# A second-product weight half in a weight room instead of a staging room, in a float32 four-layer trunk

## The chip, the core and the metric

The kernel runs on one core of one Trainium2 chip. The metric is the device time of one execution in microseconds (us). Engines are named as in the profile: PE is TensorE (PEld its weight loads), DVE is VectorE, ACT is ScalarE, POOL is GpSimd, SP is SyncE, which here only issues transfers. An engine works through its own instructions in the order in which they were recorded, and waits at an instruction until what it reads is there and the room it writes is free.

## The reference

A trunk of four layers over 512 tokens of width 1024: a mixer and a gated feed-forward in each, and a last norm.

```python
D_MODEL = 1024; SEQ = 512; DEPTH = 4
FFN_HIDDEN = -(-8 * D_MODEL // (3 * 256)) * 256          # 2816

def swiglu_ffn(h, w_gate_up, w_down):
    g, u = jnp.split(h @ w_gate_up, 2, axis=-1)
    return (jax.nn.silu(g) * u) @ w_down

def reference(x, ...):
    for layer in range(DEPTH):
        kind = layer % N_MIXERS          # 0: s5_mixer, 1: gla_mixer, 2: diff_attn_mixer
        h = rmsnorm(x, norm_mix[layer])
        ...
        x = x + mix.astype(x.dtype)
        h = rmsnorm(x, norm_ffn[layer])
        x = x + swiglu_ffn(h, ffn_w_gate_up[layer], ffn_w_down[layer]).astype(x.dtype)
    return rmsnorm(x, norm_final)
```

The change lies in `@ w_down` of the feed-forward of layers 2 and 3.

## The kernel before

**Precision.** Every float32 factor is split into a high part (a cast by ACT to the format that TensorE takes, line 420) and a low part (source minus high part, by DVE, line 428), and a product of two factors is three TensorE products: high by high, high by low, low by high. So each weight tile of 128 x 1024 that is loaded is cast once and subtracted once. The result lies in a "whl" room, of which there are five in rotation; a cast waits until TensorE has read what the room held before.

**The feed-forward.** `ffn` works through 11 blocks of 256 hidden columns. A block's gate and up halves are computed with seven products instead of eight (sums of weight quarters and of activations take the place of one). Its steps have names: one, five, six, two, seven, three, four for the products, gate2 for the scaling and silu of the second half (lines 786 and 789), times for the product of gate and up (line 748 in layer 2, 750 in layer 3) into a "raw" tile. In layer 2 the tokens stand in a turned order there, and a half of the raw tile needs both writes of times; in layer 3 the first token half is written early.

**The down groups.** In layers 2 and 3, which have no side work of earlier stages, blocks 0 to 3 and 4 to 7 are each followed by `seven_down`: their 1024 hidden columns times w_down, again by seven products (lines 1113 to 1210). The four quarters of the weights and their sums are named "11", "21", "1", "S", "3", "22"; each is two halves of 128 x 1024 (j = 0, 1). The operands from raw are named "11", "12", "2", "1", "3", "4", "22" (`parts`: a cast by ACT on line 1114, a subtraction by DVE on line 1116). The products come in this order, operand by weight, and the bank: 11 by 11 (a), 12 by 21 (d), 2 by S (a), 1 by 1 (c), 3 by 3 (a), 4 by 22 (c), 22 by S (a). A product is 24 matmuls of 128 x 512 on line 1125; its result is added to x on line 1134. So there are four groups in a run; the page and the rows call them by their times, about 1464, 1586, 1956 and 2076 us.

**Where loaded weights lie.** There are two kinds of rooms. Three *staging rooms* ("wst", line 409) serve, in rotation, whatever is split at once: a block's "11" and "3", and of a group "11", "21" and "22". A load into one waits until DVE has subtracted from what lay there three loads ago. Eight *weight rooms* hold what is kept or added to: they are a list, taken from the front by `slots.pop(0)` and given back at its end. In the trace they are called slot, halves (four rooms that held the sides) and gain. A block takes three (its "1", "22" and "21"), a group takes four at first ("1" and "S"), and two more for "3". Transfers into them are on lines 772 (blocks) and 1089 (groups); some are followed by an accumulating transfer of a second quarter on POOL's queue (lines 775 and 1098).

**The order.** Inside these layers the code is written in program order, and a scheduler places each engine's instructions by what they depend on and by that order; SP's loads can so stand far ahead of the code that asks for them, if their room is free. In `seven_down`, `weights` loads "1" and "S" while the group's last block is being computed, `sums` loads "11" and then "21" behind that block's last product, `before` splits both, and `products` does the rest: after the first product it loads "3".

Of the kernel before, what the change touches and what calls it, by code (L numbers as in the profile page):

```python
# [340 lines left out]
class Trunk:  # L341
# [730 lines left out]
    def seven_down(self, fp, slots, rooms, wd, b0, r, na, turn):  # L1072
# [4 lines left out]
        W, H, side = {}, {}, {}  # L1077
# [3 lines left out]
        def source(kh, nh):  # L1081
            return [self.wb_src(wd, at(kh, j), nh * 512) for j in range(2)]

        def load(name, kh, nh, plus=None, keep=False):
            W[name] = []
            for src in source(kh, nh):
                if keep:
                    w = slots.pop(0)[:].rearrange("p k n -> p (k n)").rearrange("p (k n) -> p k n", n=512)
                    nc.sync.dma_start(w, src)
                else:  # L1090
                    w = self.staged(src, 2, 512)[:]
                W[name].append(w)
            if plus:
                more(name, *plus)

        def more(name, kh, nh):
            for w, src in zip(W[name], source(kh, nh)):
                nc.gpsimd.dma_start(w, src, accum_op=ALU.add)

        def split(name):  # L1100
            H[name] = []
            for w in W[name]:
                hl = self.high(w, 2, 512)
                self.low(hl, w)
                H[name].append(hl)

        def freed(name):
            for w in W.pop(name):
                slots.append(w.rearrange("p k n -> p (k n)").rearrange("p (k n) -> p k n", n=256))

        def parts(name, pieces):
            side[name] = o = fp.tile([P, 2, 4, 256], F32R, tag="act", name="part", bufs=na)
            for ks, y in pieces:
                self.last["part high"] = nc.scalar.copy(o[:, 0, ks], y)
            for ks, y in pieces:
                self.last["part low"] = v.tensor_tensor(o[:, 1, ks], y, o[:, 0, ks].bitcast(F32), op=ALU.subtract)

        def product(name, w, banks, first):
            o, hls = side.pop(name), H.pop(w)
            for k in range(4):  # L1120
                hl = hls[k // 2]
                for t in range(2):
                    ts = slice(t * P, (t + 1) * P)
                    for n, (y, z) in enumerate(((0, 0), (0, 1), (1, 0))):
                        self.last["mm"] = nc.tensor.matmul(  # L1125
                            banks[t][:], o[:, y, k, ts], hl[:, z, k % 2],
                            start=first and not (k or n), stop=k == 3 and n == 2, skip_group_check=True,
                        )

        def add(m, d, banks, f):  # L1130
            for t in range(2):
                n = 2 * m + t
                xs = self.x[:, n, d * 512 : d * 512 + 512]
                v.scalar_tensor_tensor(xs, banks[t][:], f[:, n : n + 1], xs, op0=ALU.mult, op1=ALU.add)  # L1134
# [2 lines left out]
        us = []  # L1137

        def weights():
            load("1", 0, 1, (0, 0), True)  # L1140
            load("S", 1, 1, None, True)

        def early():
            parts("11", [(whole, part(0, 0))])
# [4 lines left out]

        def sums():  # L1150
            load("11", 0, 0)
            load("21", 1, 0)
            with self.tc.issue_after(self.last["low"].ins):
                for w, y in zip(W["1"], W["S"]):
                    v.tensor_tensor(y, w, y, op=ALU.add)
# [7 lines left out]
        def products():  # L1163
            self.flush()
            if turn:
                parts("12", [(whole, part(0, 1))])
                self.behind = {"silu": self.last["part high"], "scaled": self.last["part low"]}
            s1, s2, s4 = part(1, 0), part(0, 0), part(0, 1)
            for ks, y in us:
                v.scalar_tensor_tensor(s2[:, ks], y, -1.0, part(1, 1)[:, ks], op0=ALU.mult, op1=ALU.subtract)  # L1170
            self.behind = None
            a = [self.acc("a2") for _ in range(2)]
            product("11", "11", a, True)
            load("3", 0, 1, (1, 1), True)
            parts("2", [(whole, s2)])
            split("S")
            add(0, 0, a, r)
            nr = self.sp.tile([P, NT], F32, tag="ms4", name="nr", bufs=2)
            with self.tc.issue_after(self.last["part low"].ins):
                v.tensor_scalar_mul(nr[:], r[:], -1.0)  # L1180
            d = [self.sbank("d2") for _ in range(2)]
            product("12", "21", d, True)
            more("S", 1, 0)
            with self.tc.issue_after(self.last["part low"].ins):
                v.tensor_tensor(s4, s2, s4, op=ALU.add)
                v.tensor_tensor(s1, s1, part(1, 1), op=ALU.subtract)
            parts("1", [(whole, s1)])
            split("1")
            freed("1")
            load("22", 1, 1)  # L1190
            add(0, 0, d, r)
            product("2", "S", a, False)
            parts("3", us)
            split("3")
            freed("3")
            add(0, 1, a, nr)
            c = [self.acc("c2") for _ in range(2)]
            product("1", "1", c, True)
            parts("4", [(whole, s4)])
            split("22")  # L1200
            add(1, 1, c, r)
            product("3", "3", a, False)
            parts("22", [(whole, part(1, 1))])
            split("S")
            freed("S")
            add(1, 1, a, nr)
            product("4", "22", c, False)
            add(0, 1, c, r)
            product("22", "S", a, False)
            add(1, 0, a, r)  # L1210

        return {"early": early, "before": before, "sums": sums, "weights": weights, "products": products}

    def turn_x(self, r):
# [1922 lines left out]
```

## Time and profile before

| | |
|---|---|
| median of 3 runs | 2214.54 us (2212.77 to 2217.34) |
| profiled execution | 2214.04 us, its span 2212.3 us |
| busy in the span | PE 97%, PEld 88%, DVE 77%, ACT 53%, POOL 16% |
| granted TensorE clock, mean of the span | 0.996 |
| bytes moved, mean rate | 354.67 MB, 160 GB/s |
| line 1125, the groups' matmuls | 672 of the 15313 |

Rows of the time-ordered view give start and length in us, engine, line, operation, what is written from what, and in brackets the idle time of that engine ahead of it with what ended it. Rows of the chain of waits give start, length and what the chain passed through, DMA included, from a transfer's issue to its landing. Rows by stretch give for each engine the busy time and the count of instructions, then the clock that was granted to TensorE (1.00 is full speed), the share of the DMA engines' time and the rate. Matmuls overlap in their pipeline: 24 of them that are each shown as about 0.39 us follow one another every 0.23 us.

### The profile page before, as it was taken

Reading aid. Unit: us, or ns where it says so; the run is one execution under the profiler, and the core shown is the slowest. Engines: PE = TensorE matmul, PEld = TensorE weight load, DVE = VectorE, ACT = ScalarE, POOL = GpSimd, SP = SyncE. Lnnn points to the kernel's source line nnn. Section 1 sums busy time; section 2 is a strip of 40 time slices with the busy share of each in tenths; the row PEclk is TensorE's granted clock in tenths of the full one; section 3 lists DMA queues with packets and bytes.
Section 4 is the critical chain, followed back from the end, with each engine's and each line's share of the span. In section 5 each row is a group of like instructions: output and inputs, shape, how many; then the busy total and the mean of one; then the engine's idle time right before and its main releaser. Section 6 shows DMA issues by size and latency. Waiting matters only on the chain.

```text
span 2212.3 us, 38516 instructions
## 1 busy us (share of the span) xinstructions
PE 2150.6 (97%) x15313; PEld 1949.0 (88%) x15313; DVE 1702.6 (77%) x2580; ACT 1171.6 (53%) x1852; POOL 360.0 (16%) x467
## 2 busy tenths in 40 slices
PE   6999999999999999999999999999999999999998
PEld 5888989989988898999988888989899888979997
DVE  9965978777988597876745686988886975988885
ACT  8634645444665465564435786644554334655553
POOL 3401152340211010100002221211110000111100
PEclk9999999999999999999999999999999999999999
DMA  4356767665863676765337465988872555879762
GB/s 93 65 174 172 185 161 188 174 173 158 187 152 115 157 183 173 178 188 136 96 129 160 98 153 145 254 215 217 201 169 58 146 158 145 210 200 226 197 149 76
DMA packets 320101, 354.67 MB, mean 160 GB/s; under 512 B 71220, under 2 KB 253648, under 8 KB 319794
## 3 DMA queue, kind: packets, MB, share of 16 engines
q1 hardware_dynamic: 243362, 247.39, 36.6%
q0 software_dynamic: 76560, 104.82, 25.6%
q8 instruction: 121, 1.98, 0.4%
q14 instruction: 58, 0.48, 0.1%
HBM read 318.20 MB, written 18.75 MB: 152 GB/s over the span
## 4 chain that ended last, share of the span: by engine, by line
PE 77%; DVE 11%; ACT 4%; DMA 3%; issue 3%; POOL 1%; SPq 0%; DVEq 0%; POOLq 0%; ACTq 0%
PE a L594 19%; PE c L594 9%; PE acc L448 8%; PE acc L450 8%; PE acc L449 8%; PE d L594 5%; DVE whl L428 3%; PE a L1125 3%; PE y L1875 2%; PE acc L1911 2%; PE c L1125 2%; ACT whl L420 1%; PE s L2883 1%; DMA wst<-in_ffn_w_down_dram 1%; PE op L2916 1%
## 5 line engine op out<-in xcount | busy, mean ns | idle before, releaser
L428 DVE TENSOR_TENSOR whl<-wst,whl 128x1024 fp32r<-128x1024 f32 x252 | 306.5, 1222 | 196.8 <-ACT whl L420 195.4
L594 PE MATMUL a<-side,whl 128*128 128x256 f32 x3240 | 392.2, 277 | 5.1 <-DVE whl L428 3.3
L594 PEld LDWEIGHTS a<-side,whl 128*128 128x128 f32 x3240 | 378.7, 188 | 8.0 <-DVE whl L428 4.8
L420 ACT CAST whl<-wst 128x1024 fp32r<-128x1024 f32 x252 | 263.8, 1051 | 221.8 <-PE acc L450 117.0
L594 PE MATMUL c<-side,whl 128*128 128x256 f32 x2160 | 260.7, 277 | 2.0 <-DVE whl L428 1.6
L594 PEld LDWEIGHTS c<-side,whl 128*128 128x128 f32 x2160 | 252.5, 188 | 2.8 <-DVE whl L428 2.3
L428 DVE TENSOR_TENSOR whl<-slot,whl 128x1024 fp32r<-128x1024 f32 x121 | 147.2, 1221 | 45.7 <-ACT whl L420 45.6
L448 PE MATMUL acc<-whl,act 128*128 128x512 f32 x448 | 176.1, 394 | 0.5 <-ACT whl L420 0.5
L450 PE MATMUL acc<-whl,act 128*128 128x512 f32 x448 | 174.9, 390 | 0.0
L449 PE MATMUL acc<-whl,act 128*128 128x512 f32 x448 | 174.9, 390 | 0.0
L420 ACT CAST whl<-slot 128x1024 fp32r<-128x1024 f32 x121 | 126.7, 1052 | 86.7 <-DVE slot L850 29.7
L420 ACT CAST whl<-halves 128x1024 fp32r<-128x1024 f32 x103 | 107.9, 1051 | 85.9 <-DVE halves L850 43.1
L428 DVE TENSOR_TENSOR whl<-halves,whl 128x1024 fp32r<-128x1024 f32 x103 | 125.2, 1221 | 23.5 <-ACT whl L420 23.0
L594 PE MATMUL a<-sides,whl 128*128 128x256 f32 x1080 | 132.1, 278 | 1.6 <-DVE whl L428 1.0
L594 PE MATMUL d<-sides,whl 128*128 128x256 f32 x1080 | 131.7, 278 | 0.4 <-ACT whl L420 0.4
L594 PEld LDWEIGHTS a<-sides,whl 128*128 128x128 f32 x1080 | 127.8, 188 | 2.9 <-DVE whl L428 1.2
L594 PEld LDWEIGHTS d<-sides,whl 128*128 128x128 f32 x1080 | 127.7, 188 | 0.8 <-ACT whl L420 0.6
L775 POOL DMA_DIRECT2D wst<-in_ffn_w_gate_up_dram x44 | 56.9, 1294 | 295.6 <-DMA wst<-in_ffn_w_gate_up_dram 114.7
L448 PEld LDWEIGHTS acc<-whl,act 128*128 128x128 f32 x448 | 84.0, 188 | 18.7 <-ACT whl L420 0.7
L450 PEld LDWEIGHTS acc<-whl,act 128*128 128x128 f32 x448 | 84.1, 188 | 17.6
L449 PEld LDWEIGHTS acc<-whl,act 128*128 128x128 f32 x448 | 84.2, 188 | 16.6
L1125 PE MATMUL a<-whl,part 128*128 128x512 f32 x384 | 90.5, 390 | 2.2 <-DVE x L1134 1.8
(567 smaller groups left out, 4378.6 us busy)
## 6 DMA issues: line engine op xcount, KB each, us to landing
wst<-in_ffn_w_gate_up_dram SPq DMA_DIRECT2D x88, 512.0 KB, 5.3
wst<-in_ffn_w_down_dram SPq DMA_DIRECT2D x80, 512.0 KB, 4.7
slot<-in_ffn_w_gate_up_dram SPq DMA_DIRECT2D x67, 512.0 KB, 5.3
wst<-in_ffn_w_gate_up_dram POOLq DMA_DIRECT2D x44, 512.0 KB, 7.4
halves<-in_ffn_w_gate_up_dram SPq DMA_DIRECT2D x44, 512.0 KB, 5.6
wst<-in_s_w_glu_dram SPq DMA_DIRECT2D x32, 512.0 KB, 5.1
wst<-in_diff_w_qkv_dram SPq DMA_DIRECT2D x24, 512.0 KB, 3.9
slot<-in_ffn_w_gate_up_dram POOLq DMA_DIRECT2D x20, 512.0 KB, 9.3
```

What stands on the lines that cost most here:

```text
L420: self.last["high"] = self.nc.scalar.copy(hl[:, 0], w[:])
L428: self.last["low"] = self.nc.vector.tensor_tensor(hl[:, 1], w[:], hl[:, 0].bitcast(F32), op=ALU.subtract)
L448: mm(out, lh, rh, start=first, stop=False)
L449: mm(out, lh, rl, start=False, stop=False)
L450: self.last["mm"] = mm(out, ll, rh, start=False, stop=last)
L594: mm(o, *two, start=first and not (j or k or n), stop=k == 3 and n == 2, skip_group_check=True,)
L775: nc.gpsimd.dma_start(w[:], left.quarter(*plus, b), accum_op=ALU.add)
L1125: self.last["mm"] = nc.tensor.matmul(banks[t][:], o[:, y, k, ts], hl[:, z, k % 2], start=first and not (k or n), stop=k == 3 and n == 2, s ...
L1875: mm(yb[:, b], q[:, j, b], om[:, j // 2, bs(b)], start=False, stop=j == 3)
L1911: mm(accs[t][:], zT[:, m // 2, kk, t * P : (t + 1) * P], hl[:, m % 2, kk % 2], start=kk == 0 and m == 0, stop=kk == KT - 1 and m == 2,)
L2883: nc.tensor.matmul(ss[m][:], qs[:, m, ts], ks[:, m, z], start=z == 0, stop=z == 1)
L2916: nc.tensor.matmul(op[:, 0], aT[:, kt], vall[0][:, kt, j * P : (j + 1) * P], start=kt == 0, stop=kt == 3)
```

## The change

Of the weights "21" of a down group, the second half (j = 1) is loaded into a weight room, taken from the front of the list. The first half stays in a staging room. `keep`, until now yes or no for both halves, becomes the set of halves that get a weight room. The room is given back behind the group's first product in program order, before "3" takes its two. All else is the same; `freed` gets a second argument, from which half on it gives back.

```diff
-        def load(name, kh, nh, plus=None, keep=False):
+        def load(name, kh, nh, plus=None, keep=()):
             W[name] = []
-            for src in source(kh, nh):
-                if keep:
+            for j, src in enumerate(source(kh, nh)):
+                if j in keep:
                     w = slots.pop(0)[:].rearrange("p k n -> p (k n)").rearrange("p (k n) -> p k n", n=512)
                     nc.sync.dma_start(w, src)
                 else:
...
-        def freed(name):
-            for w in W.pop(name):
+        def freed(name, n=0):
+            for w in W.pop(name)[n:]:
                 slots.append(w.rearrange("p k n -> p (k n)").rearrange("p (k n) -> p k n", n=256))
...
         def weights():
-            load("1", 0, 1, (0, 0), True)
-            load("S", 1, 1, None, True)
+            load("1", 0, 1, (0, 0), (0, 1))
+            load("S", 1, 1, None, (0, 1))
...
             load("11", 0, 0)
-            load("21", 1, 0)
+            load("21", 1, 0, None, (1,))
...
             product("11", "11", a, True)
-            load("3", 0, 1, (1, 1), True)
+            freed("21", 1)
+            load("3", 0, 1, (1, 1), (0, 1))
             parts("2", [(whole, s2)])
```

Since a line is added, lines from 1174 on have a number higher by one in the kernel of the change.

SP's loads around the first group, before. wst_15272 and wst_15274 are the halves of "11", wst_15276 and wst_15278 those of "21", wst_15386 and wst_15388 those of "22"; the second of the two loads in the second row and the one into gain are "3"; lines 772 and wst_15553 belong to the next block.

```order
L409 DMA wst_15272<-in_ffn_w_down_dram 128x2x512
L1089 DMA halves_14151<-in_ffn_w_down_dram 128x2x512 x2
L409 DMA wst_15274<-in_ffn_w_down_dram 128x2x512
L772 DMA halves_14151<-in_ffn_w_gate_up_dram 128x4x256
L409 DMA wst_15276<-in_ffn_w_down_dram 128x2x512
L1089 DMA gain_13567<-in_ffn_w_down_dram 128x2x512
L772 DMA halves_14151<-in_ffn_w_gate_up_dram 128x4x256
L409 DMA wst_15278<-in_ffn_w_down_dram 128x2x512
L409 DMA wst_15386<-in_ffn_w_down_dram 128x2x512
L409 DMA wst_15388<-in_ffn_w_down_dram 128x2x512
L409 DMA wst_15553<-in_ffn_w_gate_up_dram 128x4x256
```

And in the change:

```order
L409 DMA wst_15272<-in_ffn_w_down_dram 128x2x512
L1089 DMA halves_14151<-in_ffn_w_down_dram 128x2x512 x2
L409 DMA wst_15274<-in_ffn_w_down_dram 128x2x512
L1089 DMA halves_14151<-in_ffn_w_down_dram 128x2x512
L409 DMA wst_15276<-in_ffn_w_down_dram 128x2x512
L1089 DMA gain_13567<-in_ffn_w_down_dram 128x2x512
L772 DMA halves_14151<-in_ffn_w_gate_up_dram 128x4x256
L409 DMA wst_15385<-in_ffn_w_down_dram 128x2x512
L409 DMA wst_15387<-in_ffn_w_down_dram 128x2x512
L409 DMA wst_15552<-in_ffn_w_gate_up_dram 128x4x256
L772 DMA halves_14151<-in_ffn_w_gate_up_dram 128x4x256
```

The second load of the second row is now the second half of "21". The halves of "3" are the two single loads on line 1089: the one into gain as before, the other in the room and place that the next block's "1" had. The next block's "1" has the place of its "22", and its "22" comes behind the staged loads, into the room that "21" gives up.

DVE at the same place, before. whl_15282 and whl_15285 are the low parts of "11", whl_15288 and whl_15291 those of "21", whl_15337 and whl_15340 those of "S"; part_15299 is operand "12".

```order
L428 TENSOR_TENSOR whl_15285<-wst_15274,whl_15285 128x1024
L428 TENSOR_TENSOR whl_15288<-wst_15276,whl_15288 128x1024
L878 TENSOR_TENSOR r2_15153<-c_15095,r2_15153 128x512
L748 TENSOR_TENSOR raw_15014<-r2_15153,r1_15093 128x64x4 x2
L428 TENSOR_TENSOR whl_15291<-wst_15278,whl_15291 128x1024
L786 TENSOR_TENSOR g2_15294<-a_15065,R_14598 128x512
L428 TENSOR_TENSOR whl_15337<-halves_14151,whl_15337 128x1024
L748 TENSOR_TENSOR raw_15014<-g2_15294,r5_15123 128x64x4 x2
L1170 SCALAR_TENSOR_TENSOR raw_14801<-s3_14899,raw_15014 128x2x256
L428 TENSOR_TENSOR whl_15340<-slot2_14331,whl_15340 128x1024
L1116 TENSOR_TENSOR part_15299<-raw_15014,part_15299 128x1024
```

And in the change:

```order
L428 TENSOR_TENSOR whl_15284<-wst_15274,whl_15284 128x1024
L428 TENSOR_TENSOR whl_15287<-wst_15276,whl_15287 128x1024
L878 TENSOR_TENSOR r2_15153<-c_15095,r2_15153 128x512
L428 TENSOR_TENSOR whl_15290<-halves_14151,whl_15290 128x1024
L748 TENSOR_TENSOR raw_15014<-r2_15153,r1_15093 128x64x4 x2
L786 TENSOR_TENSOR g2_15293<-a_15065,R_14598 128x512
L428 TENSOR_TENSOR whl_15336<-halves_14151,whl_15336 128x1024
L748 TENSOR_TENSOR raw_15014<-g2_15293,r5_15123 128x64x4 x2
L1170 SCALAR_TENSOR_TENSOR raw_14801<-s3_14899,raw_15014 128x2x256
L428 TENSOR_TENSOR whl_15339<-slot2_14331,whl_15339 128x1024
L1116 TENSOR_TENSOR part_15298<-raw_15014,part_15298 128x1024
```

The low part of the second half of "21" reads a weight room (halves) and stands ahead of the first pair of raw products instead of behind it; the rest keeps its order.

## The prediction

> **What bounds the kernel now.** I read the page first, then the stretches of the four seven-product down groups, then TensorE's own order of time in them, and last the chain of waits.
>
> ```profile
> span 2212.3 us, 38516 instructions
> PE 77%; DVE 11%; ACT 4%; DMA 3%; issue 3%; POOL 1%; SPq 0%; DVEq 0%; POOLq 0%; ACTq 0%
> ```
>
> TensorE carries 77% of the chain that ended last, so a change helps where TensorE stands idle or runs slowly, and nowhere else. The change touches the four groups alone. Busy times by stretch, one row for each group (us; PE, weight load, DVE, ACT, POOL busy, granted clock, DMA share, GB/s):
>
> ```profile
> 1463.60:1508.40 44.80, 40.85 (x171) 32.98 (x170) 38.37 (x44) 21.91 (x23) 6.27 (x5) 0.92 0.86 213
> 1585.70:1627.70 42.00, 40.20 (x170) 32.49 (x169) 37.50 (x43) 21.90 (x23) 6.24 (x5) 0.96 0.89 214
> 1955.90:1999.60 43.70, 40.05 (x170) 31.16 (x169) 38.20 (x43) 20.44 (x22) 6.22 (x5) 1.00 0.89 216
> 2076.30:2114.40 38.10, 38.10 (x171) 31.55 (x170) 36.87 (x41) 20.55 (x22) 6.27 (x5) 1.00 0.87 213
> ```
>
> The fourth group has no gap: seven products in 38.10 us, 5.44 us each, 0.227 us for each of 24 matmuls. Against it the first loses 6.7 us, the second 3.9, the third 5.6, together 16.2 us. That is the ceiling of any change to these waits. TensorE's rows show where it is lost (start, length, what, idle before it and what ended that):
>
> ```profile
> 1457.26 2.88 PE L594 MATMUL c<-side,whl 128*128 128x256 f32 x24
> ...
> 1463.61 5.62 PE L1125 MATMUL a<-whl,part 128*128 128x512 f32 x24
> 1473.18 8.15 PE L1125 MATMUL d<-whl,part 128*128 128x512 f32 x24 [3.95 <-ACT part L1114]
> 1481.16 5.60 PE L1125 MATMUL a<-whl,part 128*128 128x512 f32 x24
> ...
> 1592.36 1.20 PE L1125 MATMUL d<-whl,part 128*128 128x512 f32 x4 [1.07 <-ACT part L1114]
> 1594.28 6.38 PE L1125 MATMUL d<-whl,part 128*128 128x512 f32 x20 [0.73 <-DVE part L1116]
> 1600.50 5.60 PE L1125 MATMUL a<-whl,part 128*128 128x512 f32 x24
> ...
> 1965.95 2.76 PE L1125 MATMUL d<-whl,part 128*128 128x512 f32 x11 [0.76 <-DVE whl L428]
> 1970.17 0.70 PE L1125 MATMUL a<-whl,part 128*128 128x512 f32 x2 [1.47 <-DVE x L1134]
> ```
>
> All of it lies at the second product (bank d) and, in the third group, in the products behind it. The releasers named are ACT and DVE. The chain of waits says what held those:
>
> ```profile
> 1460.14 6.80 DMA wst<-in_ffn_w_down_dram
> 1467.04 1.06 ACT whl L420
> ...
> 1472.08 1.05 ACT part L1114
> ...
> 1581.33 4.74 DMA wst<-in_ffn_w_down_dram
> 1586.17 1.06 ACT whl L420
> ...
> 1955.08 8.41 DMA wst<-in_ffn_w_down_dram
> 1963.59 1.05 ACT whl L420
> ```
>
> In three groups of four the root is one transfer: the second half of weights "21". Its staging room comes free only when the first half of "11" has been split, so it starts at 1460.14 and ACT's cast of it stands until 1467.04. On ACT and DVE everything behind that cast is late with it: the last block's gate (L786), its product into raw (L748), and from that the operand "12" of the second product (L1114 and L1116).
>
> **The change part by part.** (1) *The half moves to a weight room.* SyncE's rows in the first group:
>
> ```profile
> 1435.00 3.83 SPq L1089 DMA_DIRECT2D halves<-in_ffn_w_down_dram  x2
> 1450.22 0.37 SPq L772 DMA_DIRECT2D halves<-in_ffn_w_gate_up_dram  x1
> 1454.40 0.37 SPq L1089 DMA_DIRECT2D gain<-in_ffn_w_down_dram  x1
> 1455.54 0.37 SPq L772 DMA_DIRECT2D halves<-in_ffn_w_gate_up_dram  x1
> 1460.14 3.23 SPq L409 DMA_DIRECT2D wst<-in_ffn_w_down_dram  x3
> ```
>
> The second of the two issues of the first row (1435.00 + 3.83 - 0.37 = 1438.46) was the first half of "3". In the order of the change "21"'s second half has that place and that room. It goes out 21.7 us before 1460.14; with the 6.80 us of its landing it is there by 1445.3, before any cast of it can run: the cast writes a split room that the last block's product "three" reads until 1457.26 + 2.88 = 1460.1. The transfer leaves the path entirely.
>
> (2) *What is then next on the path, first group.* DVE's rows:
>
> ```profile
> 1462.90 0.68 DVE L878 TENSOR_TENSOR r<-c,r 128x512 f32<-128x512 f32 x1
> 1463.62 1.08 DVE L748 TENSOR_TENSOR raw<-r,r 128x256 f32<-128x256 f32 x2
> 1468.12 1.23 DVE L428 TENSOR_TENSOR whl<-wst,whl 128x1024 fp32r<-128x1024 f32 x1 [3.42 <-ACT whl L420]
> 1469.27 0.68 DVE L786 TENSOR_TENSOR g<-a,R 128x512 f32<-128x512 f32 x1
> 1473.82 1.22 DVE L1116 TENSOR_TENSOR part<-raw,part 128x1024 fp32r<-128x1024 f32 x1
> ```
>
> In the new order the low half of "21" (1.15 us from start to start) stands ahead of the raw pair, right behind L878. So L786 starts at 1463.5 + 1.15 + 1.05 = 1465.7 in place of 1469.27: 3.6 us earlier. It needs the last block's product, which ends as the group begins, at 1463.6, so nothing else holds it. What follows L786 has the same order on DVE and moves with it: ACT's part "12" to 1468.5, the first matmul of d to 1469.6, the end of L1116 (1473.82 + 1.22 = 1475.04) to 1471.4. TensorE is done with the first product at 1463.61 + 5.44 = 1469.05. Of 3.95 us of idle time 0.5 stays, four matmuls run, a wait of about 1.0 for L1116 stays, and the other 20 take 20 x 0.227 = 4.5: the third product starts at 1476.0 instead of 1481.16. Gain 5.1 us.
>
> Part of that is clock. While d ran, TensorE was granted half its speed:
>
> ```profile
> 1477.00:1478.00 1.00, 1.00 (x4) 0.81 (x3) 1.00 (x3) 0.00 (x0) 0.00 (x0) 0.50 0.99 180
> ```
>
> Group averages of 0.92 and 0.96 (rows above) say that the first lost 44.8 x 0.08 = 3.6 us of clock (idle time among them) and the second 42.0 x 0.04 = 1.7; the second fell after gaps of only 1.07 + 0.73 us, the third, at 1.00, did not in spite of similar ones. I take it that the remaining 0.5 + 1.0 us does not set it off; what it costs otherwise is a rival below. The Trainium skill (TensorE: Matmul & The Clock Gate, Part 1) says that the clock falls after an idle window of about 3.4 us. The second group's rows differ from that: 1.8 us of idle time in two pieces was enough. By the page the sum is the one below, by that row up to 3.4 us less.
>
> (3) *Second group.*
>
> ```profile
> 1584.09 0.68 DVE L878 TENSOR_TENSOR r<-c,r 128x512 f32<-128x512 f32 x1
> 1588.40 0.68 DVE L786 TENSOR_TENSOR g<-a,R 128x512 f32<-128x512 f32 x1
> ```
>
> By the same step L786 starts at 1584.7 + 1.15 + 1.05 = 1586.9, 1.5 us earlier. The first matmul of d moves from 1592.36 to 1590.9, which is before TensorE is ready (1585.7 + 5.44 = 1591.1), so that gap closes; the wait for L1116 ends at 1592.8 in place of 1594.28, and 20 matmuls at full clock end at 1597.4 instead of 1600.50. Gain 3.1 us.
>
> (4) *Third group.* Its operand "12" doesn't hang on the last gate, so d starts on time; the late half stops it in its middle and puts DVE behind.
>
> ```profile
> 1957.31 1.22 DVE L428 TENSOR_TENSOR whl<-wst,whl 128x1024 fp32r<-128x1024 f32 x1
> 1964.67 1.23 DVE L428 TENSOR_TENSOR whl<-wst,whl 128x1024 fp32r<-128x1024 f32 x1 [4.41 <-ACT whl L420]
> 1969.95 1.21 DVE L1116 TENSOR_TENSOR part<-raw,part 128x1024 fp32r<-128x1024 f32 x1
> ```
>
> DVE stands 4.41 us, and from 1964.67 it sets TensorE's pace. With the half there, DVE runs through from 1957.31 and all behind is 4.4 to 4.5 us earlier: L1116 would end at about 1967.3 (one add of 0.7 us now stands ahead of it), where TensorE wants the third product at 1955.9 + 10.9 = 1966.8. The next two products keep small waits, since DVE still sets them. Gain 4.5 of the 5.6 lost.
>
> (5) *Fourth group:* nothing to gain. *Free by cover:* the half of "3" that gives up its place now starts with the room that comes free at 1450.22; the next block's first sum (that row before) takes the place of the 1455.54 row, and that one, the next block's "22", goes out after the low half of "21", about 1465. These two are used only for the next block, which TensorE begins where the group ends, at 1508.40, and "3" for the fifth product; so 6 us of transfer and, for the two sums, 6 more of accumulation lie beside TensorE's products. If that cover were gone, it is the last rival. Splits, adds and matmuls are the same in number; one staging room fewer is used in a group, so the next staged loads start no later.
>
> Sum: 5.1 + 3.1 + 4.5 + 0 = 12.7 us. Both bounds: nothing below 0 gain by this step alone, at most 16.2. Against the profiled execution's own 2214.04 us (span 2212.3) it gives 2201.3; the median of the runs lies 0.5 higher, and I round to **2202**.
>
> **The rivals.** *The clock still falls* in the first and second group: the second group's 1.7 us in each, 2202 + 3.4 = 2205. For it speaks the second group now, against it the third.
>
> *Another transfer takes its place:* the first half of "21" still goes through a staging room, and starts after the last block's "3" is split. If the traffic that is now earlier made it land 3 us later, its cast would hold the same queue; three groups would give back up to 9 us: 2211. Against: as many bytes move as before, and 21.7 us of lead is far more than was missing.
>
> *Nothing happens:* if the room were not free at 1438, or the late operand hung on the last block's gate alone, the time stays at 2214. Against: the room took a load at that moment already, and DVE's 3.42 us ended with the cast.
>
> *Slower: "3" comes late.*
>
> ```profile
> 1481.41 1.05 ACT L420 CAST whl<-halves 128x1024 fp32r<-128x1024 f32 x1 [1.69 <-PE d L1125]
> ...
> DMA to landing us min/median/max: 3.4/5.7/14.8
> ```
>
> ACT's casts of "3" come from this row's place on, which would now be 1476.3, with the operand of the product in bank c behind them on ACT. The half needs two transfers, the load from 1450.2 and the accumulation on POOL's queue behind it (1.2 us of issue). At median landings it is there at 1462.8, 13.5 us early. It decides only when the two landings pass 25 us together; with the longest, 14.8 twice, it is there at 1481.0, 4.7 us late, in all four groups 18.8: 2221.
>
> **How the numbers follow.** Forecast 0.72, clock 0.11, another transfer 0.07, nothing 0.05, slower 0.05. The likeliest gives 2202; its own range is 2198.3 (all 16.2 us) to 2205. To hold eight of ten I leave out the top of the "another transfer" case, the unchanged and the slower one: 2198 to 2210. Differences under 0.2% (4.4 us) can't be told from none here. Faster by more than that means under 2210.1: the first two cases and some of the third, 0.87. Same: 0.08. Slower: 0.05.
>
> **What would show it.** After the change the chain of waits should have no staging transfer of w_down at 1460, 1581 and 1955; ACT's cast of "21"'s second half should read from a weight room with no wait for DMA; idle time before d should be under 1 us in the first group and none in the second; the clock should read 1.00 over all four groups, and these should last about 39.7, 38.9, 39.2 and 38.1 us. Wrong it is if d's idle time stays with another releaser, if the clock falls again, or if ACT waits for the rooms of "3" at 1476.

## The result, and the profile after

The changed kernel takes 2202.94 us (median of 4 runs, 2199.88 to 2204.37), beside 2214.26 (2212.77 to 2217.34) for the kernel before: a ratio of 0.9945, 95% interval 0.9928 to 0.9962. It is faster by 8 to 16 us; 2202 was predicted. Timed twice more beside experiments it took 2202.92 (ratio 0.9944, 0.9931 to 0.9956) and 2204.16 (0.9948, 0.9936 to 0.9961). Four executions of the experiments, with a mean clock of only 0.56 to 0.77, are left out of all medians and ratios here.

The head of the page and the chain of waits by engine, of the changed kernel:

```profile
span 2198.2 us, 38512 instructions
PE 79%; DVE 12%; ACT 4%; issue 2%; DMA 2%; POOL 0%; SPq 0%; DVEq 0%; POOLq 0%; ACTq 0%
```

The span is 14.1 us shorter, with the same number of matmuls (15313). The four groups by stretch (columns as in the prediction):

```profile
1463.10:1502.70 39.60, 38.70 (x171) 31.37 (x170) 37.93 (x44) 20.95 (x22) 7.54 (x6) 1.00 1.03 255
1580.00:1618.90 38.90, 38.44 (x171) 31.51 (x170) 37.24 (x44) 21.10 (x22) 6.54 (x6) 1.00 1.02 244
1946.30:1985.50 39.20, 38.93 (x171) 31.30 (x170) 38.12 (x43) 19.84 (x21) 6.71 (x6) 1.00 1.05 252
2062.10:2100.20 38.10, 38.10 (x170) 31.56 (x169) 36.06 (x41) 20.17 (x22) 6.26 (x5) 1.00 1.00 238
```

From the first matmul of a group to the first behind it, the groups went from 44.75, 42.03, 43.70 and 38.10 us to 39.60, 38.85, 39.21 and 38.09. That is 12.8 us; the clock, 0.92 and 0.96 in the first two, is 1.00 in all. Of the other 1.3 us of the span, 0.55 lies ahead of the first group (it starts at 1463.06 in place of 1463.61) and 0.8 between the second and third, where the change has nothing; further profiled executions of the same kernel had spans of 2201.2 and 2199.9, so this is what one execution differs from the next. In the three groups the chain of waits holds no transfer of w_down any more, where the prediction had found one in each (1460, 1581 and 1955 us).

TensorE in order of time, first group, then second, then third:

```profile
1463.06 5.65 PE L1125 MATMUL a<-whl,part 128*128 128x512 f32 x24
1468.89 1.19 PE L1125 MATMUL d<-whl,part 128*128 128x512 f32 x4 [0.18 <-ACT part L1114]
1470.80 4.83 PE L1125 MATMUL d<-whl,part 128*128 128x512 f32 x20 [0.72 <-DVE part L1116]
1475.46 5.60 PE L1125 MATMUL a<-whl,part 128*128 128x512 f32 x24
...
1585.46 1.07 PE L1125 MATMUL d<-whl,part 128*128 128x512 f32 x4
1586.99 4.83 PE L1125 MATMUL d<-whl,part 128*128 128x512 f32 x20 [0.46 <-DVE part L1116]
1591.65 5.60 PE L1125 MATMUL a<-whl,part 128*128 128x512 f32 x24
...
1957.17 5.86 PE L1125 MATMUL a<-whl,part 128*128 128x512 f32 x24
1962.87 5.90 PE L1125 MATMUL c<-whl,part 128*128 128x512 f32 x24
1969.04 5.72 PE L1125 MATMUL a<-whl,part 128*128 128x512 f32 x24 [0.27 <-DVE x L1134]
```

The wait of 3.95 us ahead of bank d is 0.18, that of 1.07 is gone, and from the first matmul of d to the next product it is 6.57 us (1468.89 to 1475.46, 0.72 of them idle) instead of 7.98 (1473.18 to 1481.16). SyncE, ACT and DVE of the first group show why:

```profile
1434.83 3.83 SPq L1089 DMA_DIRECT2D halves<-in_ffn_w_down_dram  x2
...
1458.90 1.04 ACT L420 CAST whl<-wst 128x1024 fp32r<-128x1024 f32 x1
1459.84 1.05 ACT L420 CAST whl<-halves 128x1024 fp32r<-128x1024 f32 x1
...
1475.71 1.05 ACT L420 CAST whl<-gain 128x1024 fp32r<-128x1024 f32 x1 [1.66 <-PE d L1125]
1478.38 1.06 ACT L420 CAST whl<-halves 128x1024 fp32r<-128x1024 f32 x1 [0.68 <-PE a L1125]
...
1462.26 0.68 DVE L878 TENSOR_TENSOR r<-c,r 128x512 f32<-128x512 f32 x1
1462.86 1.21 DVE L428 TENSOR_TENSOR whl<-halves,whl 128x1024 fp32r<-128x1024 f32 x1
1463.99 1.09 DVE L748 TENSOR_TENSOR raw<-r,r 128x256 f32<-128x256 f32 x2
1464.91 0.68 DVE L786 TENSOR_TENSOR g<-a,R 128x512 f32<-128x512 f32 x1
...
1469.53 1.22 DVE L1116 TENSOR_TENSOR part<-raw,part 128x1024 fp32r<-128x1024 f32 x1
```

The second issue of the first row, at 1434.83 + 3.83 - 0.37 = 1438.29, is now the second half of "21". ACT casts it at 1459.84 right behind the first half, with no wait in brackets. DVE's 3.42 us in front of its low part are gone, and L786 runs 3.8 us sooner measured from the group's start (1464.91 - 1463.06 = 1.85 in place of 5.66). The two casts of "3" (gain and halves, the third and fourth ACT rows) waited for TensorE, not for a transfer.

### The profile page after: what moved, and what is told of

It is laid out like the page before. It is cut to its first block, busy times and chain, and to the rows that moved or that the text cites. A ratio compares the mean times of both kernels' runs of the same rounds, so it can differ in the third digit from the quotient of the medians.

```text
span 2198.2 us, 38512 instructions
## 1 busy us (share of the span) xinstructions
PE 2145.4 (98%) x15313; PEld 1946.0 (89%) x15313; DVE 1702.5 (77%) x2580; ACT 1173.0 (53%) x1852; POOL 360.9 (16%) x467
## 4 chain that ended last, share of the span: by engine, by line
PE 79%; DVE 12%; ACT 4%; issue 2%; DMA 2%; POOL 0%; SPq 0%; DVEq 0%; POOLq 0%; ACTq 0%
PE a L594 20%; PE c L594 9%; PE acc L448 9%; PE acc L450 9%; PE acc L449 9%; PE d L594 5%; DVE whl L428 4%; PE a L1125 3%; PE y L1876 2%; PE c L1125 2%; PE acc L1912 2%; PE s L2884 1%; ACT whl L420 1%; PE op L2917 1%; PE tp L117 1%
## 5 line engine op out<-in xcount | busy, mean ns | idle before, releaser
L428 DVE TENSOR_TENSOR whl<-wst,whl 128x1024 fp32r<-128x1024 f32 x248 | 301.6, 1221 | 184.4 <-ACT whl L420 181.4
```

The source lines that it names most:

```text
L428: self.last["low"] = self.nc.vector.tensor_tensor(hl[:, 1], w[:], hl[:, 0].bitcast(F32), op=ALU.subtract)
```

## The experiments

The theory: the one transfer came late because its staging room came free late; what counts is when it lands. The rivals put to the test: that the weight room or the lighter rotation of the staging rooms does it whenever the transfer goes out; that either half would do, or both would do more; that the clock is the larger part; that only one layer gains. Each kernel was timed beside the kernel before on the same chip.

**The transfer held back to its old moment.** The room is the change's, but one element of it is written behind the first low part of "11", and the load is asked for behind that write (it overwrites the element):

```diff
@@ split, after the change
+                if name == "11" and j == 0:
+                    with self.tc.issue_after(self.last["low"].ins):
+                        v.memset(W["21"][1][:, 0, 0:1], 0.0)
+                    nc.sync.dma_start(W["21"][1], source(1, 0)[1])
@@ sums, after the change
-            load("21", 1, 0, None, (1,))
+            a, b = source(1, 0)
+            w = slots.pop(0)[:].rearrange("p k n -> p (k n)").rearrange("p (k n) -> p k n", n=512)
+            W["21"] = [self.staged(a, 2, 512)[:], w]
```

> The half keeps its weight room, as in the change, but its transfer is made to wait for the split of the first half of "11", as it did in the staging room: one element of the room is set on VectorE behind that split, and the load goes out behind it. Theory (only the moment of the transfer counts): the four groups last again about 44, 41.5, 43.5 and 38.1 us and the time is that of before to within 3 us, 2211 to 2215; the chain of waits runs again through that load. Rival (one load fewer in the staging rotation, or the other rooms of the later loads, give the gain): the groups stay at 39.6, 38.9 and 39.2 and the time at 2203.

Measured: 2221.62 us, ratio 1.0024 (1.0013 to 1.0035), with groups of 45.79, 46.48, 46.59 and 38.36 us. The whole gain is gone, and more. SyncE, the chain of waits and TensorE of this kernel, first group:

```profile
1459.78 0.37 SPq L409 DMA_DIRECT2D wst<-in_ffn_w_down_dram  x1
1460.40 0.37 SPq L1109 DMA_DIRECT2D halves<-in_ffn_w_down_dram  x1
...
1460.40 9.79 DMA halves<-in_ffn_w_down_dram
...
1474.74 7.25 PE L1129 MATMUL d<-whl,part 128*128 128x512 f32 x24 [5.88 <-ACT part L1118]
```

The transfer went out at the old moment (1460.40, against 1460.14), but 0.62 us behind a staged load of "22" that had not stood ahead of it before, and took 9.79 us in place of 6.80. So it landed 1470.19 - 1463.24 = 6.95 us after the group's start, where it had been 1466.94 - 1463.61 = 3.33, and the wait ahead of d grew to 5.88. In the second and third group, too, it went out 0.62 us behind a staged load and took about 3 us more (7.99 in place of 4.74, 11.12 in place of 8.41). The direction is the theory's, but the time lies outside the 2211 to 2215 that it gave: the experiment held only the issue fixed, and not the landing. Nor did it hold DVE's order: L786 stands ahead of the late low part here (1464.19 and 1471.36), which is why d is 1.9 us later than before and not 3.6.

**Held back, but sooner.** The same, with the write one split earlier, ahead of the first cast of "11", so that the load goes out ahead of "22".

```diff
@@ split, against the kernel above
             for j, w in enumerate(W[name]):
+                if name == "11" and j == 0:
+                    with self.tc.issue_after(self.last["low"].ins):
+                        v.memset(W["21"][1][:, 0, 0:1], 0.0)
+                    nc.sync.dma_start(W["21"][1], source(1, 0)[1])
                 hl = self.high(w, 2, 512)
                 self.low(hl, w)
                 H[name].append(hl)
-                if name == "11" and j == 0:
-                    with self.tc.issue_after(self.last["low"].ins):
-                        v.memset(W["21"][1][:, 0, 0:1], 0.0)
-                    nc.sync.dma_start(W["21"][1], source(1, 0)[1])
```

> As in late, the second half of "21" lies in a weight room and its transfer is held back, but the write that holds it stands one split earlier on VectorE (ahead of the low part of the first half of "11", not behind it), so that the transfer goes out about 1.2 us sooner and, on SyncE, ahead of the first staged load of "22" and not behind it. If the moment of the landing sets the time: issued near 1458.8, landed after 4.7 to 6.8 us at 1463.5 to 1465.6, 1.4 to 3.5 us sooner than in the kernel before; the first group 40.5 to 43.3, the second 39 to 40.7, the third 39.5 to 42.3 us, the median 2204 to 2211. If the kind of room matters: as the change, 39.6, 38.9 and 39.2, about 2203. If whatever goes out at that moment lands as late as in late (9.8 us, not for the load ahead of it): 1468.6, groups near 46, 44 and 45, about 2218.

Measured: 2215.01 us (2212.53 to 2220.38), ratio 0.9997 (0.9988 to 1.0006): no change, where the theory had 2204 to 2211 and the shortest of 11 runs is above that. The profiled execution is the longest of them, 5.4 us above their median, with groups of 45.09, 44.58 and 45.22, so in the others they may well be shorter. Its chain and DVE in the first group, then ACT and TensorE in the third:

```profile
1461.47 6.84 DMA halves<-in_ffn_w_down_dram
...
1469.49 1.23 DVE L428 TENSOR_TENSOR whl<-halves,whl 128x1024 fp32r<-128x1024 f32 x1 [3.46 <-ACT whl L420]
1470.63 1.07 DVE L748 TENSOR_TENSOR raw<-r,r 128x256 f32<-128x256 f32 x2
1471.55 0.67 DVE L786 TENSOR_TENSOR g<-a,R 128x512 f32<-128x512 f32 x1
...
1967.69 1.04 ACT L420 CAST whl<-halves 128x1024 fp32r<-128x1024 f32 x1 [10.09 <-DMA halves<-in_ffn_w_down_dram]
1968.64 1.04 ACT L1118 CAST part<-raw 128x1024 fp32r<-128x1024 f32 x1
...
1969.74 1.22 PE L1129 MATMUL d<-whl,part 128*128 128x512 f32 x2 [3.37 <-ACT part L1118]
```

In the first group the half did land sooner: 1461.47 + 6.84 - 1466.05 = 2.26 us after the group's start, 1.07 before its old place. But L786 stands at 5.50 from the start, against 5.66: the raw pair (L748), which ran ahead of the waiting low part in the kernel before, now stands behind it and takes 0.9 of that back. In the second group the half landed 0.95 us after the start, where it had been 0.40, and the same order makes d late by 2.47 us where it was 1.07. In the third group it landed 0.74 us sooner, but operand "12" (L1118 here) is behind ACT's wait of 10.09 us, and d starts 3.37 us late where it had been on time. In the kernel before that operand was cast and subtracted ahead of the late half, as its ACT and DVE show (the half's own cast and low part stand at 1963.59 and 1964.67):

```profile
1957.43 1.06 ACT L1114 CAST part<-raw 128x1024 fp32r<-128x1024 f32 x1 [4.57 <-DVE raw L750]
...
1959.04 1.22 DVE L1116 TENSOR_TENSOR part<-raw,part 128x1024 fp32r<-128x1024 f32 x1
```

So the moment of the landing is not all: the change also alters what is queued behind the half. Its order is the better one only if the half is there.

**The other half, and both.** The first half of "21" in the weight room and the second staged; then both halves in weight rooms, so that nothing of "21" is staged.

```diff
-            load("21", 1, 0, None, (1,))
+            load("21", 1, 0, None, (0,))
...
-            freed("21", 1)
+            slots.append(W.pop("21")[0].rearrange("p k n -> p (k n)").rearrange("p (k n) -> p k n", n=256))
```

> The first half of "21" goes to the weight room and the second stays in staging. Then the staged half takes the room of the last block's "3", which comes free some 7 us before that of "11", and should land before its cast is due. Theory: as the change, 2201 to 2205, groups 39.6, 38.9, 39.2 and 38.1. Rival (the next late transfer takes the place: the load that starts when the block's "3" is split is late by a little too, and now the half that the product needs last is not the early one): one or more groups longer by over 0.5 us, ACT waiting for DMA at the second cast of "21".

```diff
-            load("21", 1, 0, None, (1,))
+            load("21", 1, 0, None, (0, 1))
...
-            freed("21", 1)
+            freed("21")
```

> Both halves of "21" in weight rooms, none in staging. Theory: the first half was in time in the change already, so nothing is gained: 2201 to 2205, and the groups within 0.3 us of 39.6, 38.9, 39.2, 38.1. Rival (the first half's staged load is the next bound, as in the second group before, where ACT waited 1.15 us for it): the second and third group are shorter by 0.5 us or more each. Other rival (eight rooms are too few for six halves and the block's three, so "3" and the next block's sums come late): longer, with ACT or DVE waiting for a DMA into a weight room.

Measured: 2202.86 us, ratio 0.9936 (0.9924 to 0.9948), groups 39.61, 38.84, 38.91 for the other half; 2203.49 us, ratio 0.9940 (0.9928 to 0.9951), groups 40.97, 38.86, 39.08 for both. It doesn't matter which half moves: the one that stays in staging then has a staging room early enough. Moving both brings nothing more; the second and third group stayed within the 0.3 us expected, the first did not. SyncE, ACT and TensorE of the kernel with both, first group:

```profile
1457.69 0.37 SPq L1089 DMA_DIRECT2D gain<-in_ffn_w_down_dram  x1
...
1467.02 1.05 ACT L420 CAST whl<-gain 128x1024 fp32r<-128x1024 f32 x1 [3.15 <-DMA gain<-in_ffn_w_down_dram]
...
1474.09 1.20 PE L1125 MATMUL d<-whl,part 128*128 128x512 f32 x4 [1.57 <-ACT part L1114]
```

The second half got the room "gain", which comes free late (its load went out at 1457.69, where the change's went out at 1438.29), and ACT waits for it as it had for the staging room: a shortage of one kind of room had begun to turn into one of the other. It cost 1.4 us, in one group. This is the rival of too few rooms, in a small size, and it shows that a weight room that comes free late costs what a staging room does.

**The clock alone.** The kernel before, with 24 matmuls of 128 x 128 that nobody reads, into a spare bank, in the gap ahead of d in the first group and 6 in the second. They keep TensorE busy and shorten no wait.

```diff
@@ products, the kernel before
             d = [self.sbank("d2") for _ in range(2)]
+            if turn:
+                with self.tc.issue_after(self.last["mm"].ins):
+                    self.warmed(6 if b0 else 24, self.tp("warm")[:].rearrange("p a b -> p (a b)"))
             product("12", "21", d, True)
```

> The kernel before, with matmuls of no use in the gap ahead of the second product in layer 2: 24 of 128x128 in the first group (about 0.11 us each, 2.7 us of a gap of 3.95) and 6 in the second (0.7 of 1.07), to keep the clock up. If the falling clock is its own part of the loss: the clock reads 1.00 in both groups, the second product runs its last 20 matmuls in 4.5 to 4.8 us, and the groups last 43.2 instead of 44.8 and 40.3 instead of 42.0, 2211 in all. If the clock has no part: 44.8 and 42.0 or longer.

Measured: 2215.06 us, ratio 0.9992 (0.9983 to 1.0001), the first groups 44.31 and 41.14 us. The kernel before by stretch, in its two slow pieces; then this kernel in the same places, and TensorE's rows of the first:

```profile
1471.00:1478.00 7.00, 4.82 (x11) 3.50 (x12) 6.97 (x11) 3.49 (x4) 2.39 (x2) 0.52 0.90 188
1594.00:1597.40 3.40, 3.12 (x7) 2.48 (x8) 3.40 (x6) 0.20 (x1) 0.68 (x1) 0.52 1.10 190
```

```profile
1472.00:1478.00 6.00, 6.00 (x53) 5.86 (x51) 5.72 (x8) 4.51 (x6) 1.20 (x1) 1.00 0.89 234
1478.00:1484.40 6.40, 5.85 (x28) 4.53 (x27) 6.40 (x9) 2.23 (x3) 1.20 (x1) 1.00 0.92 160
...
1472.71 5.52 PE L1580 MATMUL warm<-ident 128*128 128x128 f32 x48
1477.98 0.71 PE L1125 MATMUL d<-whl,part 128*128 128x512 f32 x2
1479.24 5.28 PE L1125 MATMUL d<-whl,part 128*128 128x512 f32 x22 [0.55 <-DVE part L1116]
1484.36 1.98 PE L1125 MATMUL a<-whl,part 128*128 128x512 f32 x8
```

The clock stays at 1.00, and from the first matmul of d to the next product it is 6.38 us (1477.98 to 1484.36) where it was 7.98 (1473.18 to 1481.16); in the second group 7.05 where it was 8.14. So at full clock d takes 1.6 and 1.1 us less, although it waits for L1116 there (0.55 us, and 1.19 in the second group, where the kernel before had no wait and 0.73): a slow d had hidden part of that wait. The dummy work overran the gap (24 of them are 48 records and 5.27 us, twice what was reckoned; the gap is 3.95), so the group as a whole shows little of it, and the groups expected, 43.2 and 40.3, were missed: this sizes the clock's share, and is no way to get it.

**One layer at a time.** The change in layer 2 alone (the first two groups), then in layer 3 alone.

```diff
-            load("21", 1, 0, None, (1,))
+            load("21", 1, 0, None, (1,) if turn else ())
...
-            freed("21", 1)
+            freed("21", 1 if turn else 2)
```

`turn` is set in layer 2; for layer 3 alone both lines have `not turn`.

> The change in the two groups of layer 2 alone. Theory, by the terms of the sum: 5.1 + 3.1 = 8.2 us faster than before, and the third group at 43.7 again. Rival (the gain is one of the whole rotation of rooms and not of each group): the third group is shorter too, or the first two longer than 40.

> The change in the two groups of layer 3 alone. Theory: 4.5 us faster than before, the first two groups at 44.8 and 42.0 and the third at 39.2. Rival as for layer 2; and if the fourth group has anything to give, over 4.5 us.

Measured: 2206.27 us, ratio 0.9955 (0.9943 to 0.9968), for layer 2; 2209.88 us, ratio 0.9977 (0.9968 to 0.9986), for layer 3. By stretch, layer 2 alone and then layer 3 alone, first to third group:

```profile
1463.30:1503.00 39.70, 38.71 (x170) 31.45 (x170) 38.04 (x45) 20.95 (x22) 7.54 (x6) 1.00 1.02 251
1580.30:1619.20 38.90, 38.44 (x170) 31.51 (x170) 37.24 (x44) 21.12 (x22) 6.70 (x6) 1.00 0.99 238
1946.70:1989.10 42.40, 39.80 (x171) 31.18 (x169) 38.12 (x43) 20.44 (x22) 6.22 (x5) 1.00 0.89 218
```

```profile
1464.40:1510.60 46.20, 41.23 (x170) 33.23 (x169) 38.22 (x44) 21.89 (x23) 6.75 (x6) 0.93 0.86 213
1588.00:1629.90 41.90, 40.24 (x170) 32.49 (x169) 37.47 (x43) 21.91 (x23) 6.24 (x5) 0.96 0.89 213
1958.50:1997.70 39.20, 38.97 (x171) 31.29 (x170) 38.11 (x43) 19.84 (x21) 6.43 (x6) 1.00 1.07 250
```

Each group has the change's time where the change is, and none of it where it is not. The unchanged groups differ from one execution to the next with the landing of the half: the first is 46.20 us here (landing 7.94 us) and 44.75 in the profile before (6.80), the third 42.4 (7.22) and 43.70 (8.41). In the kernel with the dummy matmuls, where layer 3 is as before, the third is 41.84 (6.87), so a third group shorter than 43.7 is no effect of the change in layer 2. Against 2216.01 us of the kernel before, the intervals are 7.1 to 12.6 us and 3.1 to 7.1; the prediction's terms for them, 5.1 + 3.1 = 8.2 and 4.5, lie inside. No group's gain needs the change in the other layer, as a sum of terms requires.

**The wait that is left.** The change, with the splits of "S" placed behind those of operand "12" in layer 2, so that DVE reaches L1116 two low parts (2.3 us) sooner.

```diff
@@ products, the change
                 self.behind = {"silu": self.last["part high"], "scaled": self.last["part low"]}
+                twelve = self.behind
...
             parts("2", [(whole, s2)])
+            self.behind = twelve if turn else None
             split("S")
+            self.behind = None
```

> The change, and in layer 2 the splits of "S" stand behind the low part of operand "12" on VectorE and behind its high part on ScalarE. This is the wait that is now last ahead of the second product (0.72 and 0.46 us in the first two groups). Theory (VectorE's order sets what is left): that wait closes, the first group lasts 38.3 to 38.9 and the second 38.1 to 38.5, about 1.3 us in all, too little for the times to tell. Rival (the splits of "S" are then late for the third product): the wait moves to the product behind, and the groups stay at 39.6 and 38.9 or grow.

Measured: 2200.54 us, ratio 0.9935 (0.9922 to 0.9949), groups 39.30, 38.38, 39.05. It was run again beside the change:

> The kernel of part12_first once more, for its time beside the change on one chip. If its gain is real: groups 39.3, 38.4 and 39.1, and a median 1 to 2 us below that of the change. If the 2.2 us between the two medians were run to run: medians within 1 us of each other.

> The change once more, beside part12_again: groups 39.6, 38.9, 39.1 and 38.1, median 2202 to 2204.

Measured: 2202.09 us (ratio 0.9944, 0.9931 to 0.9956) beside 2204.16 of the change; groups 39.31, 38.40, 39.07 beside 39.60, 38.87, 39.18. TensorE of the second time, first and second group:

```profile
1470.12 0.73 PE L1125 MATMUL d<-whl,part 128*128 128x512 f32 x2
1471.38 5.30 PE L1125 MATMUL d<-whl,part 128*128 128x512 f32 x22 [0.53 <-DVE part L1116]
...
1586.64 5.81 PE L1125 MATMUL d<-whl,part 128*128 128x512 f32 x24
```

In the second group d now runs in one piece. The first keeps 0.53 us, since L1116 still hangs on the cast in front of it (L1114), and so misses the 38.3 to 38.9 that were expected of it. The medians of this second comparison differ by 2.1 us. The means of five runs each differ by 2.1 and 1.0 us in the two comparisons, together 1.5 with an interval of about 0.1 to 2.9; the groups account for 0.9. It is the fastest of the kernels here, and by less than one comparison with the kernel before could show.

A fourth staging room, the other way to let the half start earlier, wasn't tried.

## Why the prediction was right, point by point

- **What bounds the kernel** held. The gain is in the three groups with the late transfer, and the fourth stayed at 38.1.
- **(1) The half moves.** Issued 24.8 us ahead of the group's start (1463.06 - 1438.29); 25.2 was read from the old rows. The cast has no wait for a transfer. Held back, it gave nothing.
- **(2) First group, 5.1 us: 5.15 measured.** Measured from the group's start, L786 was put at 2.1 us and stood at 1.85, the end of L1116 at 7.8 and 7.69, the third product at 12.4 and 12.40. The idle time left was 0.18 + 0.72, where 0.5 + 1.0 was forecast. Of the 5.15, 3.77 is the gap ahead of d (3.95 to 0.18) and 1.4 the shorter d (7.98 to 6.57), which is the clock's part, net of the wait of 0.72 that it uncovers; with the dummy matmuls it was 1.6. That the idle time left would not set the clock off was assumed there without a reason that the rows gave. By the rows on the clock's steps in the last section, 1.57 us of idle time in one step was not enough and 1.67 was; the 1.5 forecast lay just under that, the 0.90 measured well under.
- **(3) Second group, 3.1: 3.18 measured.** The gap before d closed; the wait for L1116 is 0.46, where the prediction's times leave 0.8 (1592.8 less 1591.1 and four matmuls).
- **(4) Third group, 4.5: 4.49 measured.** The third product stands at 10.90 from the start (10.9 predicted), and the 1.1 us still lost lie in the three products from there on (5.70, 6.17 and 5.56 us each, where 5.44 is full pace). That it fits to 0.01 us is partly luck: it holds for the execution from whose rows the term was worked out. The unchanged third group was 1.3 and 1.9 us shorter in two other profiles, and the term with it.
- **(5) The free edits.** From the end of one group to the start of the next in the same layer it is 77.34 us (77.31 before) and 76.65 (76.65 before), so the next block's loads, now later, cost nothing.
- **The sum** of 12.7 measured 12.8 in the groups. The medians differ by 11.3 in the first comparison, by 13.1 and 11.1 in the later ones.
- **The rivals.** The clock read 1.00 in all groups, so the first fell. The first half of "21" was cast at 1458.90 without a wait, so no other transfer took its place; it began to in the kernel with both halves moved. "3" did not come late. That the late operand hung on the gate alone fell too.
- **What the prediction did not see** is that step (2)'s "low half ahead of the raw pair", booked there as a delay of 1.15 us, is also a risk: with that order a half that landed 1.07 us sooner shortened the wait ahead of d by only 0.18 us (3.95 to 3.77). It did not matter, since the half goes out 21.6 us ahead of its cast (1438.29 and 1459.84).

## What to carry to other kernels

Follow the chain of waits back to the one transfer that is late, and ask which earlier load held its room; a spare room of another kind, with its load put far ahead, can be worth every wait that hangs on it, the clock that these cost included. One transfer is enough: with two moved, the second met the next shortage. Read the order too, since work placed behind an operand that is now early loses when that operand is late, so that a small lead can gain nothing where a large one gains everything.

## What the runs showed of the hardware beyond that

- The clock changed on a fixed grid, and idle time in pieces was enough to lower it. In the kernel before, read in stretches of 0.1 us, it fell at 1471.28 and 1594.16 us and rose again at 1478.10 and 1597.57; 1594.16 - 1471.28 is 36 steps of 3.413 us, and the slow pieces are two steps and one step long. In the step ahead of each fall TensorE was busy for 1.36 and 1.75 us of 3.41; the second of these held idle pieces of 1.07 and 0.60 us with four matmuls between them. No fall followed a step with 1.84 us busy (1.57 idle) in the first group of the kernel with both halves moved, on the grid of that execution's own fall at 282.91 us, nor any step of the third group before, where the least is 2.21. The Trainium skill (TensorE: Matmul & The Clock Gate, Part 1) has a free-running window of about 3.4 us, and half speed after an idle one. The grid agrees with that window; it need not be wholly idle, as the second group shows, and by these few rows about half of it was enough.
- The landing of one and the same 512 KB load varied. In the three groups it took 6.80, 4.74 and 8.41 us in the kernel before, 6.84, 6.41 and 8.89 held back and issued ahead of a staged load, and 9.79, 7.99 and 11.12 issued 0.62 us behind one. That the load ahead of it is the cause of these 3 us is argued from the order of issue alone. Without any change in its group it took 6.80 to 7.94 us in the first and 6.87 to 8.41 in the third.
- With the change the DMA engines' share in the groups rose from at most 0.89 to at least 1.00, and the rate from at most 216 to at least 238 GB/s; no row of TensorE, ACT or DVE in the groups waits for a transfer.
